# Reordering the split of weights in a hybrid decoder layer: low parts behind their sums, accumulating copies first, and three smaller moves

## The chip, the cores and the metric

The kernel runs on one core of a Trainium2 chip. The metric is the time of one execution on the device in microseconds; the time before is the median of three runs. The engines are named as in the profile: PE (TensorE, matrix products; its weight loads are PEld), DVE (VectorE), ACT (ScalarE), POOL (GpSimd) and SP (SyncE), which here only issues transfers.

## The reference

A decoder layer on 256 tokens of width 2048, all in float32. In short:

```python
h = layer_norm(ALPHA * x + 0.5 * swiglu(x, ffn1_w_in, ffn1_w_out))       # first feed-forward, width 5632
q, k, v, qi, ki, wi, rx, rg, gates = split_cols(h @ w_in)
y_attn = dsa_attention(rope(q), rope(k), v, rope(qi), rope(ki), wi)      # 64 keys of each query, by an indexer
y_rnn = rglru_branch(rx, rg, ...)                                        # short convolution, gates, linear recurrence
g_attn, g_rnn = split(sigmoid(gates))
merged = g_attn * (y_attn @ w_attn_branch) + g_rnn * (y_rnn @ w_rnn_branch)
h = layer_norm(ALPHA * h + merged @ w_out)
h = layer_norm(ALPHA * h + 0.5 * swiglu(h, ffn2_w_in, ffn2_w_out))       # second feed-forward
```

Here `swiglu(h, w_in, w_out)` is `(silu(a) * b) @ w_out`, with `a, b` the halves of `h @ w_in`.

## The kernel before

Every float32 product is made of three products of a rounded type (`F32R`): each operand is split into a high part, its rounded copy, and a low part, the rest; PE multiplies high by high, high by low and low by high. So each weight must be rounded by ACT (line 307) and subtracted by DVE (line 181) before PE can use it. The weights stream through in `pieces` of up to 1024 columns. `Weights.unit` hands PE the next piece and, at each new piece, loads pieces further ahead and splits pieces up to `AHEAD` = 4 ahead of the current one, into five buffers (`hl`).

Many blocks of 512 output columns use a scheme with seven instead of eight block products on quarters of an operand (a "chunk"). A chunk of weights (`rf`, 1024 KB) then gives four pieces, the forms of `FORMS`, and `operand` makes the sums that they need on DVE: `p1q3` a sum of 1024 columns into `ws` (line 262), `p2` one of 512 (266), `q5p7` one of 512 (269); `q4p6` needs none of its own, its operand being the results of 269 (first half) and 266 (second half). `p1q3` and `p2` round a part of the raw chunk, `q5p7` rounds `ws`.

A feed-forward has 22 blocks (`PLANS`). From block 6 on a block holds four pieces `o` of the product with `w_out`, for g tiles made earlier (`FILLS`), and 16 others: in three blocks out of four, four fast chunks; in the fourth, three chunks and two plain pieces `c`. At the end of a block `gate` adds its partial sums on DVE (lines 1209 to 1217, after ACT's copy in 1208), applies Silu on ACT, multiplies, and some pieces later transposes the result on PE and splits it into `g`. When four `o` pieces of an output block are done, `fill` copies two accumulators to `yd` on ACT (1250) and adds them to DRAM by a POOL transfer.

Some `o` pieces are `far`: they take no work of DVE. ACT writes a negated copy of the raw tile's half (207), a transfer on POOL's queue adds the weights to it from DRAM (208), which gives the low part, and ACT makes the rounded copy (212). A far piece has four such steps; `far_to` takes one step at each new piece, beginning 14 pieces ahead, and `far_steps` holds one generator for each piece, so that a piece is finished before the next begins.

PE, SP and POOL always run their instructions in the order of the program. DVE and ACT follow a planner's order, except in blocks 2 to 21 of each feed-forward (`WRITTEN`), where their order is the program's too. In these blocks `W.behind` is 1: the low part of a piece is put off until the next piece's sum and rounding have been issued (`lows`, `low_to`). Outside them `behind` is 0.

After the first feed-forward, `consts` computes in small steps the tables of the rotation and the constants of the recurrence (`hba`, `hbx`, `sp2`, `sp4`), while the last output product and the norm run. Later `merge` transposes each block of the merged branches and splits it (`split_two`) for the product with `w_out`; the last block (`nb` 3) is needed by the first block of that product.

Of the kernel before, what the change touches and what calls it, by code (L numbers as in the profile page):

```python
# [11 lines left out]
AF = mybir.ActivationFunctionType  # L12
# [130 lines left out]
class Weights:  # L143
# [8 lines left out]
    def __init__(self, nc, pool, pieces, on_piece):  # L152
        self.nc, self.pool, self.on_piece = nc, pool, on_piece
        self.fast_pool = self.third = None
        self.chunks = 0
        self.wide = None
        self.pieces = pieces
        self.raw = {}
        self.sums = {}
        self.hl = {}  # L160
        self.loaded = 0
        self.split = 0
        self.cur = -1
        self.limit = None
        self.cap = len(pieces)
        self.off = 0
        self.far = []
        self.soon = ()
        self.apart = ()
        self.far_raw = {}  # L170
        self.far_loaded = self.far_split = 0
        self.far_steps = deque()
        self.lows = deque()
        self.behind = 0

    def low_to(self, n):


        while len(self.lows) > n:
            lp, src, hp = self.lows.popleft()  # L180
            self.last = self.nc.vector.tensor_tensor(lp, src, hp, op=OP.subtract)  # L181

    def far_to(self, i):


        nc = self.nc
        while (self.far_loaded < len(self.far) and
               self.far[self.far_loaded] <= i + FAR_LOADS[self.far[self.far_loaded] in self.soon]):
            k = self.far[self.far_loaded]
            ap = self.pieces[k][0]  # L190
            t = self.far_raw[k] = self.pool.tile([P, PIECE], F32, name=f"raw{k}", tag="raw", bufs=RAW_BUFS)
            nc.sync.dma_start(t, ap)
            self.far_loaded += 1
        while self.far_split < len(self.far) and self.far[self.far_split] <= i:
            k = self.far[self.far_split]
            ap, t = self.pieces[k][0], self.far_raw.pop(k)
            self.far_split += 1
            self.far_steps.append((k, self.far_copies(k, ap, t)))
        if self.far_steps:
            self.far_step()  # L200

    def far_copies(self, k, ap, t):
        nc = self.nc
        h, l = [], []
        for c in range(2):
            l.append(self.wide())
            nc.scalar.activation(l[c], t[:, c * 512:(c + 1) * 512], AF.Copy, scale=-1.0)
            nc.gpsimd.dma_start(l[c], ap[:, c * 512:(c + 1) * 512], accum_op=OP.add)
            yield
        for c in range(2):  # L210
            h.append(self.wide())
            nc.scalar.activation(h[c], t[:, c * 512:(c + 1) * 512], AF.Copy)
            if c == 0:
                yield
        self.hl[k] = (h, l)

    def far_step(self):
        if next(self.far_steps[0][1], self) is self:
            self.far_steps.popleft()

    def key(self, i):
        ap, form = self.pieces[i]
# [55 lines left out]
    def split_to(self, i, step=PIECE):  # L278
        nc = self.nc
        while self.split <= min(i, len(self.pieces) - 1):  # L280
            form = self.pieces[self.split][1]
            if self.split in self.far:
                self.split += 1
                continue
            self.load_to(self.split)
            k = self.key(self.split)
            if self.split in self.apart:
                h, l = ([self.wide() for _ in range(2)] for _ in range(2))
                for c in range(2):
                    src = self.raw[k][:, c * 512:(c + 1) * 512]  # L290
                    nc.scalar.activation(h[c], src, AF.Copy)
                    nc.vector.tensor_tensor(l[c], src, h[c], op=OP.subtract)
                self.hl[self.split] = (h, l)
                del self.raw[k]
                self.split += 1
                continue
            hl = self.pool.tile([P, HL_PITCH], F32R, name=f"hl{self.split}", tag="hl", bufs=HL_BUFS)
            o = self.begin(self.split)
            h, l = hl[:, o:o + PIECE], hl[:, o + PIECE:o + 2 * PIECE]
            n = self.size(self.split)  # L300
            if form:
                parts = [(self.operand(k, form), *(x[:, :n].rearrange("p (f r c) -> p f r c", r=2, c=256)
                                                   for x in (h, l)))]
            else:
                parts = [tuple(x[:, q:min(n, q + step)] for x in (self.raw[k], h, l)) for q in range(0, n, step)]
            for src, hp, lp in parts:
                nc.scalar.activation(hp, src, AF.Copy)  # L307
                self.lows.append((lp, src, hp))
                self.low_to(self.behind)
            self.hl[self.split] = (h, l)  # L310
            if form in (None, FORMS[-1]):
                del self.raw[k]
            self.split += 1

    def unit(self, n):
        if self.cur < 0 or self.off == self.size(self.cur):
            self.hl.pop(self.cur, None)
            self.cur += 1
            self.off = 0
            self.far_to(self.cur + EARLY)  # L320
            while self.far_steps and self.far_steps[0][0] <= self.cur:
                self.far_step()
            self.load_to(self.cur + AHEAD + LOADS)
            self.split_to(self.limit or min(self.cur + AHEAD, self.cap))
            self.on_piece(self.size(self.cur) * (1 if self.pieces[self.cur][1] else 2))
        h, l = self.hl[self.cur]
        o = self.off
        self.off += n
        assert self.off <= self.size(self.cur)
        if self.cur in self.apart or self.cur in self.far:  # L330
            return h[o // 512], l[o // 512]
        return h[:, o:o + n], l[:, o:o + n]
# [80 lines left out]
def tile_layer(ctx, tc, x_fm, x_tm, pos, f1a, f1o, wA, wki, wB, wG, lru, wab, wrb, wo, f2a, f2o,  # L413
# [193 lines left out]
    def consts():  # L607
# [9 lines left out]
        for dst, turn, shift in ((sn, 0.0, 0.0), (cs, 0.25, 1.5707963267948966)):  # L617
            k = SM(32)
            r = SM(32)
            V.tensor_scalar(k, ang, 0.15915494309189535, turn, op0=OP.mult, op1=OP.add)  # L620
            V.tensor_scalar(k, k, 12582912.0, None, op0=OP.add)
            V.tensor_scalar(k, k, 12582912.0, None, op0=OP.subtract)
            V.scalar_tensor_tensor(r, k, -6.28125, ang, op0=OP.mult, op1=OP.add)
            V.scalar_tensor_tensor(r, k, -0.0019350051879882812, r, op0=OP.mult, op1=OP.add)
            yield
            V.scalar_tensor_tensor(r, k, -3.019916050195849e-07, r, op0=OP.mult, op1=OP.add)
            V.tensor_scalar(r, r, shift, None, op0=OP.add)
            V.tensor_scalar(r, r, 3.1415925, -3.1415925, op0=OP.min, op1=OP.max)
            angles.append((dst, r))
            yield  # L630
        o, w = COLS["ba"]
        V.tensor_scalar(hba, cols[:, o:o + w], 0.5, None, op0=OP.mult)
        o, w = COLS["bx"]
# [11 lines left out]
        V.tensor_scalar(n, ya, 1.4426950408889634, 12582912.0, op0=OP.mult, op1=OP.add)  # L645
        V.tensor_scalar(n, n, 12582912.0, None, op0=OP.subtract)
        yield
        with tc.issue_after(split.last.ins):
            for dst, r in angles:
                A.activation(dst.rearrange("p a b -> p (a b)"), r, AF.Sin)  # L650
        r = SM(NR)
        V.scalar_tensor_tensor(r, n, 0.693359375, ya, op0=OP.mult, op1=OP.subtract)
        V.scalar_tensor_tensor(r, n, -0.00021219444005469057, r, op0=OP.mult, op1=OP.add)
# [546 lines left out]
    def ffn(x, forms, ln):  # L1200
        def gate(c, e, g, i, lag, plain, steps):
# [4 lines left out]
            if e:  # L1206
                p1, p6, p7, q5 = e[0][:, :S], e[0][:, S:], e[1][:, :S], e[1][:, S:]
                A.activation(z4[:, 0], p1, AF.Copy)
                V.tensor_tensor(z4[:, 1], z4[:, 0], p6, op=OP.add)
                if lag != LAG_T[1]:  # L1210
                    W.low_to(0)
                V.tensor_tensor(z4[:, 2], z4[:, 1], p7, op=OP.add)
                V.tensor_tensor(b, q5[:, None, :].to_broadcast([P, 2, S]), z4[:, 1:3], op=OP.subtract)
                for t in range(2):
# [39 lines left out]
        for s, (b0, b1) in enumerate(SEGS):  # L1254
            for n in range(b0, b1):
                if n == WRITTEN[0]:
                    ordered.enter_context(tc.manual_schedule(
                        engines={mybir.EngineType.DVE, mybir.EngineType.Activation}))
                    W.behind = 1
                if n == NBK - 1:  # L1260
                    W.cap = W.cur + len(PLANS[n]) + 2
                c, e = blockF(x, forms, PLANS[n], fill)
# [3 lines left out]
                    next(task)  # L1266
                W.cap = len(pieces)
                bg.add("gate", task)
        W.behind = 0
        W.low_to(0)  # L1270
        ordered.close()

        def back():
# [311 lines left out]
        return r  # L1585

    bg.add("rope", indexer(1))
    for h in range(NH):
        bg.add("head", head(h), 4, PIECE)
    for b in range(6):  # L1590
# [106 lines left out]
    def merge(s, nb):  # L1697
# [3 lines left out]
        for c2 in range(2):  # L1701
            ps = BP()
            for c in range(2):
                for t in range(2):
                    T.transpose(ps[:, c * S + t * P:c * S + (t + 1) * P],
                                s[t][:, (2 * c2 + c) * P:(2 * c2 + c + 1) * P], ident)
            mg[4 * nb + 2 * c2], mg[4 * nb + 2 * c2 + 1] = split_two("mg", ps)

    for nb in range(4):
        if nb == 2:  # L1710
# [105 lines left out]
```

## Time and profile before

| | us |
|---|---|
| median of three runs (lowest to highest) | 2291.48 (2288.58 to 2291.97) |
| profiled execution: time | 2290.86 |
| profiled execution: span, first to last instruction | 2289.1 |
| PE busy | 2235.5 |
| DVE busy | 2146.3 |
| ACT busy | 1553.1 |
| POOL busy | 307.5 |

The granted PE clock is 0.998 of full speed. By time the first feed-forward's blocks run to about 650 us, its output product and norm to 705; the projections and attention to about 1160, the recurrence to about 1400, the branch products to 1500, the output product and the second norm to 1610, and the second feed-forward's blocks to about 2235. Matrix products are pipelined, so a row shows one of 256 columns as 0.28 us long, though one starts every 0.11 us; 512 columns show 0.38 and start every 0.22. On DVE and ACT successive instructions overlap in the same way by some 0.1 us. In a row of the timeline the bracket gives the engine's idle time before the instruction and what ended it; in a row of the waits stand the total, the number of times and the longest.

### The profile page before, as it was taken

How to read it: one execution, taken by the hardware profiler on the slowest of the kernel's cores; microseconds unless marked ns; L12 is line 12 of the kernel's file. 1: busy time of each engine (PE TensorE's matmuls, PEld its weight loads, DVE VectorE, ACT ScalarE, POOL GpSimd, SP SyncE). 2: the span in 40 equal slices, each digit the busy share in tenths (PEclk: the TensorE clock that was granted, in tenths of full speed). 3: DMA queues.
4: the chain of work that ended last, by engine and by line, in shares of the span. 5: the costliest groups of instructions: out<-in, count | busy, mean ns of one | idle time of the engine just before them, and what ended most of it. 6: DMA issues, size and time to landing. Idle time of an engine off the chain costs nothing.

```text
span 2289.1 us, 39930 instructions
## 1 busy us (share of the span) xinstructions
PE 2235.5 (98%) x15214; PEld 2071.1 (90%) x15214; DVE 2146.3 (94%) x3121; ACT 1553.1 (68%) x2270; POOL 307.5 (13%) x416
## 2 busy tenths in 40 slices
PE   9999999999999999999999999999999999999998
PEld 7999999999988999889999998888889899999997
DVE  8999999999989999979988889998999999999997
ACT  7666777777757656566557885546667677777773
POOL 1111222222210000000100002100111122222211
PEclk9999999999999999999999999999999999999999
DMA  9878999898966555664676668756787899999975
GB/s 364 260 223 233 293 270 294 249 295 256 300 223 220 197 175 204 217 203 147 248 250 205 208 193 306 256 186 212 265 272 216 247 265 279 272 270 294 268 236 205
DMA packets 150959, 559.52 MB, mean 244 GB/s; under 512 B 17616, under 2 KB 18384, under 8 KB 127856
## 3 DMA queue, kind: packets, MB, share of 16 engines
q1 hardware_dynamic: 102672, 455.00, 55.2%
q0 software_dynamic: 47952, 101.85, 21.9%
q8 instruction: 119, 1.95, 0.3%
q14 instruction: 72, 0.59, 0.1%
q10 hardware_dynamic: 144, 0.13, 0.0%
HBM read 519.69 MB, written 37.22 MB: 243 GB/s over the span
## 4 chain that ended last, share of the span: by engine, by line
PE 36%; DVE 24%; issue 6%; DMA 2%; ACT 1%; POOL 0%; DVEq 0%; ACTq 0%; POOLq 0%
PE mm L802 20%; DVE hl L181 12%; PE mm L1479 9%; PE bp L802 6%; DVE ws L262 3%; DMA wd<-f2o 1%; DVE rf L266 1%; DVE rf L269 1%; ACT hl L307 1%; PE bp L1479 1%; DVE z L1217 1%; DMA rf<-wrb 0%; DVE y L777 0%; DVE y L775 0%; DVE stg L1369 0%
## 5 line engine op out<-in xcount | busy, mean ns | idle before, releaser
L307 ACT ACTIVATE hl<-rf 128x1024 fp32r<-128x1024 f32 x537 | 484.4, 912 | 249.5 <-DVE rf L269 128.9
L181 DVE TENSOR_TENSOR hl<-rf,hl 128x1024 fp32r<-128x1024 f32 x537 | 557.8, 1040 | 2.4 <-ACT hl L307 1.9
L181 DVE TENSOR_TENSOR hl<-raw,hl 128x1024 fp32r<-128x1024 f32 (+2 forms) x403 | 475.0, 1190 | 52.7 <-ACT hl L307 50.9
L307 ACT ACTIVATE hl<-raw 128x1024 fp32r<-128x1024 f32 (+2 forms) x403 | 410.6, 1032 | 164.4 <-PE mm L802 113.9
L802 PE MATMUL mm<-hl,hs 128*128 128x512 f32 (+1 forms) x2532 | 498.5, 337 | 11.8 <-DVE hl L181 6.7
L802 PEld LDWEIGHTS mm<-hl,hs 128*128 128x128 f32 x2532 | 410.0, 190 | 56.4 <-DVE hl L181 9.1
L802 PE MATMUL bp<-hl,sh 128*128 128x256 f32 x2148 | 429.6, 276 | 0.4 <-DVE hl L181 0.4
L802 PEld LDWEIGHTS bp<-hl,sh 128*128 128x128 f32 x2148 | 354.6, 192 | 1.4 <-DVE hl L181 0.6
L802 PE MATMUL mm<-wd,g 128*128 128x512 f32 x1176 | 267.2, 379 | 6.6 <-DMA wd<-f2o 4.2
L802 PE MATMUL bp<-hl,sl 128*128 128x256 f32 x1074 | 258.4, 275 | 0.0
L802 PEld LDWEIGHTS mm<-wd,g 128*128 128x128 f32 x1176 | 218.1, 189 | 39.7 <-DMA wd<-f2o 6.5
L802 PE MATMUL mm<-hl,xs 128*128 128x256 f32 (+1 forms) x1272 | 231.6, 316 | 15.0 <-DVE hl L181 8.9
L262 DVE TENSOR_TENSOR ws<-rf 128x1024 f32<-128x1024 f32 x179 | 218.3, 1220 | 8.7 <-DMA rf<-wrb 3.7
L307 ACT ACTIVATE hl<-ws 128x1024 fp32r<-128x1024 f32 x179 | 188.7, 1054 | 52.5 <-DVE ws L262 16.6
L802 PEld LDWEIGHTS mm<-hl,xs 128*128 128x128 f32 x1272 | 193.3, 192 | 30.9 <-DVE hl L181 11.6
L1479 PE MATMUL mm<-hs,hl 128*128 128x256 f32 x1920 | 219.5, 275 | 0.0
L181 DVE TENSOR_TENSOR hl<-ws,hl 128x1024 fp32r<-128x1024 f32 x179 | 218.0, 1218 | 1.2 <-ACT hl L307 1.1
L802 PE MATMUL mm<-hl,g 128*128 128x512 f32 (+1 forms) x936 | 212.9, 381 | 4.8 <-DVE hl L181 4.3
L1479 PEld LDWEIGHTS mm<-hs,hl 128*128 128x128 f32 x1920 | 216.6, 192 | 0.3
L802 PEld LDWEIGHTS bp<-hl,sl 128*128 128x128 f32 x1074 | 206.1, 192 | 0.8
L802 PEld LDWEIGHTS mm<-hl,g 128*128 128x128 f32 x936 | 173.5, 191 | 29.3 <-DVE hl L181 5.5
L802 PE MATMUL mm<-hl,sh 128*128 128x256 f32 x716 | 158.4, 275 | 0.0
(278 smaller groups left out, 3060.2 us busy)
## 6 DMA issues: line engine op xcount, KB each, us to landing
rf<-f1a SPq DMA_DIRECT2D x70, 1024.0 KB, 8.0
rf<-f2a SPq DMA_DIRECT2D x70, 1024.0 KB, 8.1
raw<-f1o SPq DMA_DIRECT2D x88, 512.0 KB, 8.1
raw<-f2o SPq DMA_DIRECT2D x88, 512.0 KB, 7.9
raw<-wB SPq DMA_DIRECT2D x80, 512.0 KB, 4.9
raw<-wG SPq DMA_DIRECT2D x54, 512.0 KB, 4.6
wd<-f1o POOLq DMA_DIRECT2D x92, 256.0 KB, 9.0
wd<-f2o POOLq DMA_DIRECT2D x92, 256.0 KB, 8.9
```

The source lines that it names most:

```text
L181: self.last = self.nc.vector.tensor_tensor(lp, src, hp, op=OP.subtract)
L262: v.tensor_tensor(t, b[:, 0:4:3], b[:, 1:2].to_broadcast([P, 2, 2, 256]), op=OP.add)
L266: v.tensor_tensor(b[:, 1], t[:, 1], b[:, 0], op=OP.add)
L269: v.tensor_tensor(b[:, 0], b[:, 1], b[:, 2], op=OP.add)
L307: nc.scalar.activation(hp, src, AF.Copy)
L802: T.matmul(o, x, m, start=start, stop=stop)
L1217: V.tensor_tensor(zt, zt, c[t][:, :w], op=OP.add)
L1479: T.matmul(ps.rearrange("p (k e) -> p k e", e=2), w, x.rearrange("p (e k) -> p k e", e=2), start=start, stop=stop)
```

## The change

- `low_to`, `lows` and `behind` go: each low part is issued directly after its own sum and rounding, in the written blocks too, and `gate` no longer has one between its sums.
- The rounding of the form `q4p6` becomes two ACT instructions of half the size, the second half of the operand first.
- `far_steps` becomes two queues, one of negated copies with their accumulating transfers, one of rounded copies. Each step takes from the first as long as there is something in it. Still one step for each new piece, and all steps of a piece before it is current.
- `consts` ends after the rotation's tables. The rest is the generator `lru_consts`, begun with the attention heads, beside the gate products.
- The split of the last merged block is issued under `tc.high_priority()`.

```diff
@@ Weights
-        self.far_steps = deque()
-        self.lows = deque()
-        self.behind = 0
-    def low_to(self, n):
-        while len(self.lows) > n:
-            lp, src, hp = self.lows.popleft()
-            self.last = self.nc.vector.tensor_tensor(lp, src, hp, op=OP.subtract)
+        self.far_steps = deque(), deque()
@@ far_to, for each far piece that comes within reach
-            self.far_steps.append((k, self.far_copies(k, ap, t)))
+            h, l = self.hl[k] = [None] * 2, [None] * 2
+            for c in range(2):
+                part = slice(c * 512, (c + 1) * 512)
+                self.far_steps[0].append((k, self.far_low, (l, c, t[:, part], ap[:, part])))
+                self.far_steps[1].append((k, self.far_high, (h, c, t[:, part])))
+    def far_low(self, l, c, src, ap):
+        l[c] = self.wide()
+        self.nc.scalar.activation(l[c], src, AF.Copy, scale=-1.0)
+        self.nc.gpsimd.dma_start(l[c], ap, accum_op=OP.add)
+    def far_high(self, h, c, src):
+        h[c] = self.wide()
+        self.nc.scalar.activation(h[c], src, AF.Copy)
+    def far_step(self, until=None):
+        for steps in self.far_steps:
+            while steps and (until is None or steps[0][0] <= until):
+                _, step, args = steps.popleft()
+                step(*args)
+                if until is None:
+                    return
@@ split_to
-                nc.scalar.activation(hp, src, AF.Copy)
-                self.lows.append((lp, src, hp))
-                self.low_to(self.behind)
+                for r in (1, 0) if form == FORMS[-1] else (slice(None),):
+                    nc.scalar.activation(hp[:, r], src[:, r], AF.Copy)
+                self.last = nc.vector.tensor_tensor(lp, src, hp, op=OP.subtract)
@@ consts, and a new generator behind it
+    def lru_consts():
         o, w = COLS["ba"]
         V.tensor_scalar(hba, cols[:, o:o + w], 0.5, None, op0=OP.mult)
...
@@ gate
                 V.tensor_tensor(z4[:, 1], z4[:, 0], p6, op=OP.add)
-                if lag != LAG_T[1]:
-                    W.low_to(0)
                 V.tensor_tensor(z4[:, 2], z4[:, 1], p7, op=OP.add)
@@ ffn
-                    W.behind = 1
...
-        W.behind = 0
-        W.low_to(0)
@@ attention
     bg.add("rope", indexer(1))
+    bg.add("main", lru_consts())
@@ merge
-            mg[4 * nb + 2 * c2], mg[4 * nb + 2 * c2 + 1] = split_two("mg", ps)
+            with tc.high_priority() if nb == 3 else nullcontext():
+                mg[4 * nb + 2 * c2], mg[4 * nb + 2 * c2 + 1] = split_two("mg", ps)
```

More of the change, by code (lines that the diff above doesn't have):

```diff
@@ L197, in far_to @@
             self.far_split += 1
-            self.far_steps.append((k, self.far_copies(k, ap, t)))
[L199 to L219, printed above, removed]
+            h, l = self.hl[k] = [None] * 2, [None] * 2
[3 more added lines that the diff above has]
+                self.far_steps[1].append((k, self.far_high, (h, c, t[:, part])))
+        self.far_step()
+    def far_low(self, l, c, src, ap):
[12 more added lines that the diff above has]
+                    return
     def key(self, i):
@@ L320, in unit @@
             self.far_to(self.cur + EARLY)
-            while self.far_steps and self.far_steps[0][0] <= self.cur:
-                self.far_step()
+            self.far_step(self.cur)
             self.load_to(self.cur + AHEAD + LOADS)
@@ L630, in consts @@
             yield
+        with tc.issue_after(split.last.ins):
+            for dst, r in angles:
+                A.activation(dst.rearrange("p a b -> p (a b)"), r, AF.Sin)
+    def lru_consts():
         o, w = COLS["ba"]
@@ L647, in consts @@
         yield
-        with tc.issue_after(split.last.ins):
-            for dst, r in angles:
-                A.activation(dst.rearrange("p a b -> p (a b)"), r, AF.Sin)
         r = SM(NR)
```

## The prediction

> **What bounds the kernel now.** I read the windows of the two long feed-forward stretches first, then the waits of PE and of DVE inside them, then the timeline rows in which PE or DVE sat idle.
>
> ```profile
> core 0: us, PE busy (x) PEld busy (x) DVE busy (x) ACT busy (x) POOL busy (x), PEclk, DMA share, GB/s
> 60.00:650.00 590.00, 577.87 (x4084) 541.84 (x4082) 571.94 (x668) 432.43 (x605) 120.89 (x140) 1.00 0.90 262
> 1640.00:2215.00 575.00, 561.36 (x3961) 525.22 (x3959) 562.21 (x658) 422.26 (x593) 116.98 (x134) 1.00 0.91 268
> PE mm L802 <- DVE hl L181: 11.1, 15, 2.2
> PE mm L802 <- DMA wd<-f1o: 1.3, 2, 1.0
> PE mm L802 <- DVE hl L181: 6.7, 12, 1.3
> PE mm L802 <- DMA wd<-f2o: 4.2, 4, 1.5
> DVE hl L181 <- ACT hl L307: 5.3, 5, 1.6
> DVE z L1209 <- ACT z L1208: 8.5, 8, 2.0
> ```
>
> Half of the run lies in these two stretches, and there PE (98%) and DVE (97%) are both nearly full, ACT (73%) is not. PE lacks 12.1 us in the first and 13.6 in the second, DVE 18.1 and 12.8. So no gain here can pass 25.7 us, and it comes only if the idle time of the two engines is made to coincide less. The wait rows (two of PE in the first stretch, two of PE in the second, two of DVE in the first; the first stretch is taken to 655 there) say what PE lacks: mostly the low part (L181), then the accumulated copies (wd). The timeline shows where:
>
> ```profile
> 170.98 0.49 PE L802 MATMUL mm<-hl,xs 128*128 128x256 f32 x2 [1.32 <-DVE hl L181]
> 202.97 0.49 PE L802 MATMUL mm<-hl,xs 128*128 128x256 f32 x2 [1.32 <-DVE hl L181]
> 326.18 0.49 PE L802 MATMUL mm<-hl,xs 128*128 128x256 f32 x2 [0.85 <-DVE hl L181]
> 357.02 0.49 PE L802 MATMUL mm<-hl,xs 128*128 128x256 f32 x2 [0.84 <-DVE hl L181]
> 418.19 0.49 PE L802 MATMUL mm<-hl,xs 128*128 128x256 f32 x2 [0.35 <-DVE hl L181]
> 652.10 8.90 PE L802 MATMUL mm<-hl,g 128*128 128x512 f32 x40 [2.17 <-DVE hl L181]
> 401.15 0.42 DVE L1209 TENSOR_TENSOR z<-z,bp 128x256 f32<-128x256 f32 x1 [2.03 <-ACT z L1208]
> 401.49 1.22 DVE L181 TENSOR_TENSOR hl<-rf,hl 128x1024 fp32r<-128x1024 f32 x1
> 402.63 0.41 DVE L1212 TENSOR_TENSOR z<-z,bp 128x256 f32<-128x256 f32 x1
> 415.79 1.22 DVE L262 TENSOR_TENSOR ws<-rf 128x1024 f32<-128x1024 f32 x1
> 416.92 1.22 DVE L181 TENSOR_TENSOR hl<-rf,hl 128x1024 fp32r<-128x1024 f32 x1
> ```
>
> The gaps repeat once a block, at one place: the last two products of a q4p6 form, which need its low part. In the DVE rows that low part (416.92) stands behind the next chunk's first sum (415.79); the two starts lie 1.13 us apart, and PE's gap of 0.35 ends at 418.19, as the low part does. The other loss is at a block's end: DVE waits 2.03 us for the first gate sum (401.15) while a low part that is already rounded stands behind it (401.49).
>
> **The change part by part.** The sum is made against the profiled execution, 2290.86 us (span 2289.1), 0.6 below the median shown, 2291.48.
>
> *1. Low parts directly behind their sums.* In blocks 2 to 21 of both feed-forwards the same DVE instructions run in another order. At the gap the low part comes one sum (1.13) earlier. At a block's end where DVE is idle, a second low part (1.13) moves into the idle time ahead of the gate sum. Together 2.27 us of lead over the walk from one place to the other. From the second I take off 0.4, because that low part will itself wait for its rounding, so 1.9. Is the lead used up? A cycle is four blocks, three with four fast chunks and one with three. Gap to gap a block takes 357.02-326.18 = 30.84, of which PE idles 0.85: DVE loses about 0.85 on PE with each fast block, 2.5 over three, and the fourth gives it back. A lead of 1.9 therefore covers all but some 0.3 to 0.8 of a cycle's gaps; take 0.5 left. In the first cycle (170.98, 202.97) a block takes 31.99 and PE idles 1.49 of it (1.32 and one smaller gap), 4.5 in three blocks; there the lead saves 1.9 and the rest stays, since DVE has no idle time to give. The two stretches have 8.9 (11.1 less the 2.17 at 652.10) and 6.7 us of such gaps: 4.5 each are the first cycle's, 6.6 the six later cycles'. Gain: 2 x 1.9, and 6.6 - 6 x 0.25 (half of what is left was DMA's, below) = 5.1. Together 8.9; bounds 0 (DVE's work per block is unchanged, so where it has no idle time nothing need come) and 15.6 (all).
>
> The price is a wait that was hidden: a low part that follows its own sum waits for ACT where ACT is late. The place is the block's fill end:
>
> ```profile
> 395.83 1.09 ACT L1250 ACTIVATE yd<-mm 128x512 f32<-128x512 f32 x2 [1.64 <-PE mm L802]
> 397.90 1.23 DVE L181 TENSOR_TENSOR hl<-raw,hl 128x1024 fp32r<-128x1024 f32 x1 [0.87 <-ACT hl L307]
> ACT hl L307 <- DVE rf L269: 128.9, 110, 3.7
> L307 ACT ACTIVATE hl<-rf 128x1024 fp32r<-128x1024 f32 x358 | 375.2, 1056 | 206.4 <-DVE rf L269 128.9 <-PE mm L802 52.7 <-PE bp L802 13.9
> L307 ACT ACTIVATE hl<-rf 128x512 fp32r<-128x512 f32 x179 | 111.9, 625 | 43.0 <-PE mm L802 40.4 <-PE mm L785 1.7 <-PE bp L802 0.5
> ```
>
> ACT's copies to yd wait for PE, and the next rounding stands behind them. Now DVE has a sum to do meanwhile; afterwards it waits up to one sum (1.13) more. There are 40 pairs of such copies. Mostly PE is then the late one and the lead of 1.9 bears it, so I take a net 3 us of loss, between 0 and 40 x 1.13 = 45.
>
> *2. The last form rounded in halves.* The rounding of q4p6 waits for the sum at L269 (128.9 us, 110 times). Half of its operand is ready a sum earlier, so only the second half (625 ns) is left behind that sum, and it ends within the low part of the form before (1.22): without halves, 1056 ns would barely fit. That removes a new wait of part 1 more than one of today. Cost: 179 x (2 x 625 - 1056) = 35 us of ACT work at most, in an engine that idles 27%. Zero, 0 to 2.
>
> *3. Negated copies ahead of rounded ones.* Two far pieces lie side by side; the second one's negated copies now come before the first one's rounded copies, two steps earlier.
>
> ```profile
> 1915.04 0.62 ACT L207 ACTIVATE wd<-raw 128x512 fp32r<-128x512 f32 x1
> 1918.14 0.63 ACT L207 ACTIVATE wd<-raw 128x512 fp32r<-128x512 f32 x1
> 1919.15 1.59 POOL L208 DMA_DIRECT2D wd<-f2o x1
> 1935.11 0.70 PE L802 MATMUL mm<-wd,g 128*128 128x512 f32 x2 [1.22 <-DMA wd<-f2o]
> DMA to landing us min/median/max: 4.0/9.0/16.2
> SPq L248 <- ACT wd L212: 15.4, 5, 6.2
> SPq L248 <- DVE hl L181: 484.5, 74, 14.9
> ```
>
> PE's gap at 1935.11 is at the last two products of the second far piece, whose second negated copy ran at 1918.14; its accumulating DMA is POOL's row at 1919.15, issued behind two yd stores, and lands 16 us later. The copy would take the place of a rounded one some 4 us earlier, and POOL would issue it ahead of the yd stores. The longest such wait is 1.5, so these gaps (1.3 + 4.2) should go: 5.5. I count 5.0 (0 to 6). The same number of copies runs on ACT, and POOL issues as many DMAs. The rounded copies come later, but still several pieces ahead of PE. The raw tile of the first piece is freed two steps later, so SP's queue, where a load waits for it five times (15.4), waits some 3 us more at each; that is covered, as SP waits 484.5 us for DVE anyway. If that cover goes, a load of rf is late next and DVE's first sum waits for it.
>
> The Trainium skill, DMA: Bandwidth & Descriptors, section on the anatomy of one DMA issued from GpSimd, fits a single transfer as a fixed 2 us plus its bytes over 436 GB/s; for 256 KB that is an estimate of 2.6 us. By it the copy of 1918.14 would have landed near 1923, no order of copies would matter, and this term would be 0. The landing row above, median 9.0, disagrees, and the measurement decides.
>
> *4. The last merged tile split with priority.*
>
> ```profile
> 1507.42 1.04 PE L1705 MATMUL bp<-ident,gf 128*128 128x128 f32 x8
> 1514.35 0.63 ACT L707 ACTIVATE sh<-sf 128x512 fp32r<-128x512 f32 x1 [3.23 <-DVE sf L705]
> 1515.83 1.07 ACT L956 ACTIVATE mg<-bp 128x512 fp32r<-128x512 f32 x2
> 1516.46 0.48 PE L802 MATMUL mm<-hl,mg 128*128 128x512 f32 x1 [2.82 <-ACT mg L956]
> 1517.83 9.51 PE L802 MATMUL mm<-hl,mg 128*128 128x512 f32 x35 [0.89 <-DVE mg L957]
> ```
>
> The transposes end at 1508.5, but ACT copies them only at 1515.83, after it sat 3.23 us behind a subtraction of another task. Put first, the copies end near 1509.6 and DVE's halves near 1511, ahead of PE's need at 1513.6: 3.7 goes. ACT's roundings move back by 1.07 and DVE's low parts by 1.3, which five buffers ahead cover. Gain 3.3 (0 to 3.7). Late next is the low part of a weight piece.
>
> *5. The recurrence constants beside the gates.*
>
> ```profile
> 685.75 0.18 DVE L675 TENSOR_TENSOR s<-s,s 128x20 f32<-128x20 f32 x1
> 689.53 1.12 PE L1007 MATMUL bp<-ident,y 128*128 128x128 f32 x8 [0.81 <-DVE y L1027]
> ```
>
> By the code 49 tiny DVE instructions leave the end of the first feed-forward; each 0.18, so up to 9 us of DVE. A few stand within the norm's chain ahead of the gap of 0.81. Gain 0.5 (0 to 1.5). They land in the gate products, where heads and low parts leave DVE idle in the trace; 0 (a loss of up to 1).
>
> *6. Ends of the feed-forwards.* At 652.10 PE waits 2.17 for a low part behind the gate sums, which stand behind another low part. That one now runs earlier; DVE's sums end about 0.7 sooner. Twice: 1.4 (0 to 2.2).
>
> Sum: 8.9 - 3 + 0 + 5.0 + 3.3 + 0.5 + 1.4 = 16.1 of gain. 2290.86 - 16.1 = 2274.8; on the scale of the median 2275.4. I predict 2275.
>
> **Rivals.**
> *A, slower.* The hidden wait of part 1 is paid in full: at each block's fill DVE stands a whole sum behind ACT. For it: 0.87 at 397.90, already exposed with a sum in front. Against it: only 5.3 us of such waits in the first stretch. Price 45 us, less the 19.1 of gains: 2291.5 + 26 = 2317. It decides from 19.1/40 = 0.48 us a pair; at 0.6 the time is 2296.
> *B, half of it.* The new order only swaps the gate wait for a rounding wait, and DVE's work per block, 30.84 where PE needs 30.0, keeps setting the blocks' pace. Then part 1 nets 2 and the DMA gaps, in which DVE now catches up, turn into low part gaps (2 instead of 5): 9 us of gain, 2282.5.
> *C, no change.* The stretches stay DVE's altogether and part 1's price eats part 3; parts 4 to 6 alone, less a loss from another order of ACT and DVE outside the written blocks: 2288 or so.
>
> **How the numbers follow.** 0.2% is 4.6 us, about what a measurement of this kernel can tell from no change: faster is below 2286.9, slower above 2296.1. Forecast 0.56 (its own range 2268 to 2280), B 0.22, C 0.13, A 0.09. Faster is the forecast, B and a little of C: 0.80; same most of C and the mild end of A: 0.13; slower 0.07. The range runs from 2265, near where all gaps named (15.6 + 6 + 3.7 + 1.5 + 2.2 = 29) less a price of 3 would go, to 2288, which leaves out A and half of C.
>
> **What would show it.** Right: the low part starts directly behind its own sum; the gaps of 0.85 at q4p6 are gone and the 1.32 ones smaller; no PE gap on wd; mg copied right behind the transposes; the wait of L1209 for ACT smaller. Wrong: DVE's waits for ACT's rounding in the two stretches grow past 20 us, PE's gaps at low parts stay near 15, or DVE's first sums begin to wait for rf loads.

## The result and the profile after

The changed kernel takes 2271.26 us (2269.62 to 2280.3), the kernel before 2290.69 (2288.58 to 2291.97) beside it: a ratio of 0.9925, 95% interval 0.991 to 0.9939. Forecast were 2275 and a gain of 16; it is 19.4. The profiled execution has a span of 2268.8 us, 20.3 less than before.

The page of the changed kernel, busy times (before: PE 2235.5, DVE 2146.3, ACT 1553.1 us with 2270 instructions):

```profile
PE 2230.7 (98%) x15214; PEld 2070.9 (91%) x15214; DVE 2134.7 (94%) x3121; ACT 1580.2 (70%) x2449; POOL 306.2 (13%) x416
```

ACT has 179 instructions more, the second halves, and 27 us more work. The same windows of the two feed-forwards as in the prediction, and the waits of DVE and PE in the first (60 to 655, the first four lines) and the second (the last two); a wait row is: engine, tile, line <- what ended it: us in all, times, the longest.

```profile
60.00:650.00 590.00, 585.99 (x4135) 550.85 (x4134) 575.97 (x696) 448.61 (x680) 120.30 (x140) 1.00 0.91 269
1640.00:2215.00 575.00, 567.75 (x4033) 533.50 (x4032) 563.10 (x665) 439.21 (x670) 120.32 (x141) 1.00 0.91 266
DVE hl L302 <- ACT hl L301: 11.9, 16, 1.5
PE bp L796 <- DVE hl L302: 2.9, 9, 0.4
PE mm L796 <- DVE z L1209: 0.3, 1, 0.3
DVE z L1203 <- ACT z L1202: 0.3, 1, 0.3
DVE hl L302 <- ACT hl L301: 8.9, 13, 1.2
PE bp L796 <- DVE hl L302: 3.2, 10, 0.4
```

PE now lacks 4.0 and 7.3 us (12.1 and 13.6 before). Its waits for low parts fell from 11.1 to 2.9 and from 6.7 to 3.2; those for wd are gone (its largest wait left in the second is 2.2 for g, 0.5 before); DVE's gate wait fell from 8.5 to 0.3; DVE's wait for roundings rose from 5.3 to 11.9. Where the time came from is read from PE's transposes, which both kernels issue in one order. Before, then after: ends of two blocks four blocks apart, the last gate transposes of the first feed-forward, the first norm (its row of before, 689.53, stands in the prediction), the start of the second feed-forward's norm output, and the last gate transposes of the second.

```profile
288.80 0.60 PE L1233 MATMUL bp<-ident,z 128*128 128x128 f32 x4
411.66 0.60 PE L1233 MATMUL bp<-ident,z 128*128 128x128 f32 x4
660.84 0.60 PE L1233 MATMUL bp<-ident,z 128*128 128x128 f32 x4
1600.63 1.04 PE L1041 MATMUL bp<-ident,y 128*128 128x128 f32 x8
2248.75 0.60 PE L1233 MATMUL bp<-ident,z 128*128 128x128 f32 x4
```

```profile
287.44 0.60 PE L1225 MATMUL bp<-ident,z 128*128 128x128 f32 x4
407.11 0.60 PE L1225 MATMUL bp<-ident,z 128*128 128x128 f32 x4
648.31 0.60 PE L1225 MATMUL bp<-ident,z 128*128 128x128 f32 x4
676.20 1.04 PE L1001 MATMUL bp<-ident,y 128*128 128x128 f32 x8
1590.81 1.04 PE L1035 MATMUL bp<-ident,y 128*128 128x128 f32 x8
2226.80 0.60 PE L1225 MATMUL bp<-ident,z 128*128 128x128 f32 x4
```

The first feed-forward gains 12.5 us, the second 12.1 (the lead grows from 9.8 to 21.95), the first norm 0.8; the stretch from there to the second feed-forward loses 3.5 (13.3 to 9.8), and the tail 1.65 (the spans differ by 20.3). Between the first and the last gate transposes of each feed-forward PE's idle time falls from 14.2 to 4.0 and from 15.8 to 7.3, 18.8 of these 24.6 us. The granted clock enters two of the figures: the run of 2280.3 us had 0.987 where the other three had 0.997 to 0.998, and in the profile of before it was 0.50 for 3.4 us from 2239 on, in a last block that took 34.75 us where the same block of the first feed-forward took 33.06, so that 1.7 of the second one's 12.1 is the clock's.

The gain is not the same in each cycle of four blocks. The cycle shown (blocks 10 to 13) takes 119.67 us instead of 122.86, 3.2 less. A block is taken here from the transposes behind the block before to its own, and blocks are counted from 0. By such rows the first cycle (6 to 9) gains 1.3 in each feed-forward, the next two 3.2 each in the first and 2.6 and 2.4 in the second, and the last four blocks 4.8 and, without the clock's 1.7, 4.9.

### The profile page after: what moved, and what is told of

It is laid out like the page before. It is cut to its first block, busy times and chain, and to the rows that moved or that the text cites. A ratio compares the mean times of both kernels' runs of the same rounds, so it can differ in the third digit from the quotient of the medians.

```text
span 2268.8 us, 40241 instructions
## 1 busy us (share of the span) xinstructions
PE 2230.7 (98%) x15214; PEld 2070.9 (91%) x15214; DVE 2134.7 (94%) x3121; ACT 1580.2 (70%) x2449; POOL 306.2 (13%) x416
## 4 chain that ended last, share of the span: by engine, by line
PE 40%; DVE 20%; issue 5%; ACT 2%; DMA 1%; POOL 0%; DVEq 0%; ACTq 0%; POOLq 0%
PE mm L796 24%; DVE hl L302 10%; PE mm L1468 7%; PE bp L796 7%; DVE ws L255 2%; DVE rf L262 1%; ACT hl L301 1%; DVE rf L259 1%; DMA raw<-f2o 1%; PE bp L1468 1%; DMA ya<-yd 0%; DVE stg L1358 0%; DVE sl L702 0%; ACT f L1024 0%; PE bp L1225 0%
## 5 line engine op out<-in xcount | busy, mean ns | idle before, releaser
L301 ACT ACTIVATE hl<-rf 128x1024 fp32r<-128x1024 f32 x716 | 516.8, 734 | 185.0 <-PE mm L796 71.3
L301 ACT ACTIVATE hl<-ws 128x1024 fp32r<-128x1024 f32 x179 | 188.9, 1056 | 76.0 <-DVE ws L255 46.7
```

The lines of the kernel that those rows point to most:

```text
L301: nc.scalar.activation(hp[:, r], src[:, r], AF.Copy)
```

## The experiments

**One part alone.** The kernel before with the low parts directly behind their sums, q4p6 rounded whole:

```
-                    W.behind = 1        # stays 0: nothing lags
```

> The kernel before with one edit: each low part directly behind its own sum in the written blocks (q4p6 still rounded whole, copies in the old order, constants and merge as before). Theory L (the order of DVE carries the gain of the feed-forwards): PE's gaps at low parts fall from 8.9 and 6.7 us to under 4 each, the gaps on wd stay, the two feed-forwards together get some 13 us shorter, so about 2278. Theory C (the earlier accumulating copies carry it): under 4 us of gain, above 2286. Theory P (the hidden wait for the rounding is a real price, which only the halves take away): DVE's waits for ACT's rounding in the two stretches rise above 20 us and the time is 2285 or more.

2291.35 us, ratio 0.9999 (0.9989 to 1.0009): nothing. The halves alone, low parts left one behind:

```
-                nc.scalar.activation(hp, src, AF.Copy)
+                for r in (1, 0) if form == FORMS[-1] else (slice(None),):
+                    nc.scalar.activation(hp[:, r], src[:, r], AF.Copy)
```

> The kernel before with one edit: q4p6 rounded in halves, low parts still one sum behind. Theory J (halves and direct low parts work only together: the lag already hides the rounding): within 2 us of the kernel before. Rival (ACT's late rounding costs by itself and the halves carry the gain): 8 us or more faster, 2283 or less.

2290.48 us, ratio 0.9993 (0.9983 to 1.0002): nothing either. Both edits together:

> The run above plus the rounding of q4p6 in halves. Theory L as forecast: the halves cost and gain nearly nothing, within 3 us of the run above. Theory P: at least 6 us faster than the run above, with DVE's waits for ACT's rounding that much smaller.

2271.57 us, ratio 0.9907 (0.9892 to 0.9922): about 20 us, the whole gain of the change. Two parts that are worth nothing apart are worth 20 together. The reason stands in DVE's timeline, and not in the list of waits. A chunk before, then the same in the changed kernel with the rounding on ACT (start, duration):

```profile
418.06 0.68 DVE L266 TENSOR_TENSOR rf<-ws,rf 128x512 f32<-128x512 f32 x1
418.66 1.22 DVE L181 TENSOR_TENSOR hl<-rf,hl 128x1024 fp32r<-128x1024 f32 x1
419.91 0.69 DVE L269 TENSOR_TENSOR rf<-rf 128x512 f32<-128x512 f32 x1
```

```profile
412.60 1.22 DVE L302 TENSOR_TENSOR hl<-rf,hl 128x1024 fp32r<-128x1024 f32 x1
413.74 0.68 DVE L259 TENSOR_TENSOR rf<-ws,rf 128x512 f32<-128x512 f32 x1
414.34 0.69 DVE L302 TENSOR_TENSOR hl<-rf,hl 128x512 fp32r<-128x512 f32 x1
414.94 0.68 DVE L262 TENSOR_TENSOR rf<-rf 128x512 f32<-128x512 f32 x1
415.54 1.22 DVE L302 TENSOR_TENSOR hl<-ws,hl 128x1024 fp32r<-128x1024 f32 x1
415.66 0.63 ACT L301 ACTIVATE hl<-rf 128x512 fp32r<-128x512 f32 x1 [0.29 <-DVE rf L262]
416.68 1.22 DVE L302 TENSOR_TENSOR hl<-rf,hl 128x1024 fp32r<-128x1024 f32 x1
```

A row of 1.22 is normally followed after 1.13 to 1.14 (412.60 to 413.74): neighbours overlap by 0.09. Before, the sum at L269 overwrites, in rf, what the low part right ahead of it reads; it starts only when that has ended, 1.25 behind it (418.66 to 419.91). Neither row shows a wait, and both count as busy throughout. In the changed order two 512-column instructions lie between (413.74 and 414.34). The Trainium skill, Perfetto Trace Analysis, section on the per-instruction lifecycle of a DVE or Act instruction, says that the next instruction may begin its prefetch once the one before has finished executing, while a semaphore is signalled only when the writes are acknowledged, where the profiler ends the row; the 1.13 and 1.25 agree. Another page of the Trainium skill, VectorE: DVE Perf Modes, section on the DRAIN you can't avoid, measured that a semaphore behind each of eight copies costs nothing extra; it doesn't say that one copy needed another's data, and here a neighbour that needs to wait for the one ahead costs 0.12 us.

And the first part alone, in the same place:

```profile
413.57 0.69 DVE L269 TENSOR_TENSOR rf<-rf 128x512 f32<-128x512 f32 x1
414.18 1.22 DVE L181 TENSOR_TENSOR hl<-ws,hl 128x1024 fp32r<-128x1024 f32 x1
414.38 1.06 ACT L307 ACTIVATE hl<-rf 128x1024 fp32r<-128x1024 f32 x1 [1.80 <-DVE rf L269]
415.47 1.23 DVE L181 TENSOR_TENSOR hl<-rf,hl 128x1024 fp32r<-128x1024 f32 x1
```

The whole rounding starts 0.12 behind the sum's end and ends at 415.44; the low part starts at 415.47, 1.29 behind its neighbour. So 0.155 is lost here in place of the 0.12 there, and by the account below some 0.16 at 119 such places, 19 us. Again no row shows a wait, as the low part ahead ended only 0.07 before.

To count this, I took for each two neighbouring DVE rows of the two stretches (60 to 640, 1640 to 2200; rows that the listing joins left out) the distance of their starts, less the usual distance behind a row of that form (the lowest tenth in the changed kernel), and added up what is over 0.04 us, by cause:

| us of DVE lost | behind a neighbour's read or write | gate sums | roundings | other | all | time |
|---|---|---|---|---|---|---|
| before | 19.6 | 17.8 | 4.6 | 1.2 | 43.2 | 2290.7 |
| low parts direct | 0 | 1.0 | 39.7 | 0.7 | 41.4 | 2291.4 |
| halves alone | 18.9 | 17.6 | 4.9 | 0 | 41.4 | 2290.5 |
| both | 0 | 1.0 | 24.5 | 0.5 | 26.0 | 2271.6 |
| changed | 0 | 1.0 | 21.5 | 0.6 | 23.1 | 2271.3 |

The figures are good to about 1.5 us, by which they move when the usual distance is taken a little differently. The column "all" and the time move together: 17.2 and 20 us from before to both, 20.1 and 19.4 to the changed kernel, and nearly nothing for either part alone. In part this is arithmetic. In each of the cycles of blocks 10 to 17 DVE runs the same instructions, 117.0 to 117.8 us of them in all these kernels, and the cycle lasts for these plus what DVE loses, whichever engine makes it wait. So the account says where the time went, and it doesn't prove which loss set the pace. In the changed kernel PE idles only 0.4 of the 119.7 us of such a cycle: there PE sets the pace, and the 2.3 us that DVE still loses cost next to nothing.

**Does the neighbour's overlap carry time by itself?** The changed kernel with p2's low part moved behind the next sum, so that two sums of which the second reads what the first wrote stand side by side:

```
+                self.lows.append((lp, src, hp))
+                while self.lows and form != "p2":
+                    lp, src, hp = self.lows.popleft()
                     self.last = nc.vector.tensor_tensor(lp, src, hp, op=OP.subtract)
```

> The changed kernel, with the low part of p2 moved behind the sum of q5p7, so that two sums of which the second reads what the first wrote stand next to each other on DVE in each chunk; the low part of p2 runs one 512-column instruction (0.60 us) later, all else as in the changed kernel. Theory K, overlap: the second sum starts only after the first has ended, 0.72 us behind its start instead of 0.60, in some 128 chunks of the two stretches: 15 us of DVE time, in stretches where DVE is 98% full: 2283 (2278 to 2288). Theory S (only the place of the low parts counts): a low part that comes 0.6 us later, several pieces ahead of its use, costs nothing: 2271 (2269 to 2273).

2280.80 us, ratio 0.9956 (0.9939 to 0.9973): 9.5 slower than the changed kernel's 2271.26. Its timeline:

```profile
332.03 0.69 DVE L260 TENSOR_TENSOR rf<-ws,rf 128x512 f32<-128x512 f32 x1
332.75 0.69 DVE L263 TENSOR_TENSOR rf<-rf 128x512 f32<-128x512 f32 x1
333.36 0.69 DVE L306 TENSOR_TENSOR hl<-rf,hl 128x512 fp32r<-128x512 f32 x1
334.10 0.49 PE L800 MATMUL mm<-hl,xs 128*128 128x256 f32 x2 [0.77 <-DVE hl L306]
```

0.72 between the sums, 0.61 between the unrelated neighbours. By the account, 119 such pairs lose 14.3 us, the roundings 5 less than in the changed kernel, all 33.6: 10.5 more than there, for 9.5 us of time. Theory K's number came out, but the run doesn't isolate its cause. The edit also puts the low part of p2 later, by 0.72 (a sum of 0.60 and the 0.12), and that is where PE now waits: the low part of 333.36 ends at 334.05, and PE's gap of 0.77 ends at 334.10. 25 of PE's gaps in the two stretches, 16.5 us of some 21, end so, 18 of them with 0.77; in the changed kernel no gap of PE ends with p2's low part. So theory S's "several pieces ahead of its use" was wrong, and the delay has a price of its own.

Blocks 6 and 7 show the pairs alone: there DVE loses 0.48 us a block, all of it to four pairs, and a block takes 31.93 us, where the changed kernel loses 0.31 to roundings and takes 31.75. Where DVE waits for nothing else, the time of a pair is time of the kernel. How the 9.5 us divide between pairs and delay stays open.

**The opposite test missed.** The kernel before with only q4p6's low part one behind, which parts the pair at L269 without the halves:

```
-                self.low_to(self.behind)
+                self.low_to(self.behind if form in (None, FORMS[-1]) else 0)
```

> The kernel before, in which only the last form's low part (q4p6) still goes one step behind, past the next chunk's first sum; the low parts of p1q3, p2 and q5p7 stand directly behind their own sums. q4p6 is rounded whole. Theory K, overlap: in the trace of before the sum at L269 overwrites what the low part directly ahead of it reads, and the two starts lie 1.252 us apart, 90 times in the two stretches, where the same low part ahead of an unrelated instruction (L266) takes 1.135: 0.117 lost each time, shown as no wait. Here no such pair is left at L269, and no new wait for a rounding comes, since q4p6's rounding still has a whole sum to hide behind. DVE loses 10.5 us less in the two stretches, and the time falls by 8 to 13: 2281 (2278 to 2284). Theory S, the prediction's reading (PE's gaps come because q4p6's low part stands behind the next chunk's first sum): that low part stays exactly there, so the gaps stay: 2291 (2289 to 2293).

2298.77 us, ratio 1.0031 (1.002 to 1.0041): slower, against both theories. The pairs at L269 are gone (3.9 us of neighbours' loss is left, at ws), but DVE meets another wait. DVE and ACT at the block's feed of g, and PE's wait for low parts in 60 to 640:

```profile
322.57 1.23 DVE L181 TENSOR_TENSOR hl<-ws,hl 128x1024 fp32r<-128x1024 f32 x1
322.77 1.06 ACT L307 ACTIVATE hl<-rf 128x1024 fp32r<-128x1024 f32 x1 [2.26 <-DVE rf L269]
323.74 0.58 ACT L956 ACTIVATE g<-bp 128x512 fp32r<-128x512 f32 x1
324.35 0.69 DVE L957 TENSOR_TENSOR g<-bp,g 128x512 fp32r<-128x512 f32 x1 [0.56 <-ACT g L956]
PE mm L802 <- DVE hl L181: 11.3, 10, 1.9
```

DVE's subtraction for g waits for ACT's copy of g, and this stands behind q4p6's rounding. 24 times 0.65 us are 15.6 us; roundings take 16.7, and all of DVE's loss is 44.5, 1.3 over before. That says why nothing was gained. PE's waits for low parts, nearly all for q4p6's, grew besides, from 8.9 to 11.3 in this window and from 6.7 to 10.3 in the second stretch: theory S named the place rightly, and was too low. In the profiled executions, which lie 4.8 us apart (2295.65 and 2290.86), the two feed-forwards are 1.8 and 2.2 us longer from the first to the last gate transposes, and PE idles 1.7 and 3.2 more in them. Why the medians differ by 7 stays open.

**The order of the copies.** The kernel before with part 3 alone (negated copies of all far pieces in one queue ahead of the rounded ones, as in the change's diff):

> The kernel before with one edit: negated copies with their accumulating transfers ahead of the rounded copies. Theory L: PE's gaps on wd (1.3 and 4.2 us) vanish, but in them DVE caught up, so part of them comes back as gaps at low parts: 2 to 4 us faster, about 2288. Theory C: 10 us or more faster, 2281 or less.

2291.33 us, ratio 0.9996 (0.9986 to 1.0005). Its waits of PE in 60 to 640, and that of "both", where the copies are still in the old order:

```profile
PE mm L803 <- DVE hl L181: 10.6, 15, 1.3
```

```profile
PE mm L803 <- DMA wd<-f1o: 3.0, 3, 2.5
```

The waits for wd are gone, 1.3 us, and the waits for low parts went from 8.9 in this window to 10.6: refilled, as DVE is late. In its trace the two feed-forwards are 1.7 and 0.3 us shorter than before and the stretch between them is longer, so a gain too small for the interval (3 us) is not excluded. In "both" PE waits for wd 2.5 us at one place; the changed kernel has no such wait. The changed kernel's last gate transposes of the first feed-forward lie 2.4 earlier (648.31, 650.74 in "both", which had begun 0.3 ahead), and its second feed-forward is 0.4 shorter. So part 3 is worth some 3 us once DVE is no longer late, and nothing that the times show before. The changed kernel without part 5, below, takes 2267.47, 4.1 less than "both", for parts 3 and 4 together.

**The constants.** The changed kernel without part 5:

```
-    bg.add("main", lru_consts())         # its body back at the end of consts()
```

> The changed kernel with the recurrence constants computed where they were, behind the rotation tables at the end of the first feed-forward. Theory H (the planner hoists the 47 small instructions into the projections, where DVE is full, and they cost PE time there): the projections get some 4.8 us shorter, the first norm some 0.9 longer, about 2267. Rival (the loss in the projections is another order of the planner's and not the constants): within 1.5 us of the changed kernel, 2271.

2267.47 us, ratio 0.9891 (0.9876 to 0.9906): part 5 costs 3.8. One window of the projections, before, then changed, then the latter's two largest gaps of PE, and one of the moved instructions:

```profile
760.00:930.00 170.00, 168.09 (x1341) 161.54 (x1340) 168.28 (x303) 103.19 (x138) 3.30 (x6) 1.00 0.60 211
```

```profile
760.00:930.00 170.00, 164.16 (x1297) 156.45 (x1296) 169.14 (x331) 101.64 (x145) 2.71 (x5) 1.00 0.56 196
804.40 2.40 PE L796 MATMUL mm<-hl,hs 128*128 128x512 f32 x10 [1.49 <-DVE bias L1418]
837.00 2.40 PE L796 MATMUL mm<-hl,hs 128*128 128x512 f32 x10 [1.90 <-DVE stg L1358]
L673 DVE TENSOR_SCALAR sp<-s x1: 169/169/169, 862.7 to 862.7; 128x20 f32<-128x20 f32 x1
```

The planner ran 47 of the 49 small instructions between 793.4 and 862.8, in the projections, where DVE is busy 99% of the time, and not beside the gate products for which the program names them. PE lost 3.9 us of busy time there, as theory H held. Held back until the feed-forward's last split instruction:

```
+    bg.add("main", later(lru_consts(), W.last.ins))
```

> The changed kernel with the recurrence constants held back: none of their instructions may be issued before the low part that was last when the gate products begin. Theory H (the planner's early place costs the projections, the place itself is free): the projections regain some 4.8 us and the first norm keeps its 0.9, so 2266, a little under the run with the constants put back (2267.5). Rival (the gate products have no room for them either): 2269 or more.

2268.04 us, ratio 0.9897 (0.9882 to 0.9912): the same as with the constants in their old place. The projections are free again and the gates pay some 2.

**The last merged tile.** In addition a pause of two steps of the background task that splits mg's sums, so that in the program its rounding stands behind mg's copies:

```
+            for _ in range(pause if k == 0 else 0):   # pause=2 for mg
+                yield
```

> As the run above, and the left operands of the merged tiles, whose rounding holds ACT up, wait two steps more after the first pair, so that ACT's copies of the last merged block stand ahead of them in the program. Theory M (priority did nothing because the copies stood behind instructions issued earlier in the program; the stall is ACT's order): PE's gaps of 2.8 and 0.6 to 0.9 at the last merged block fall below 1 together, 2.5 to 3.5 us faster than the run above. Rival (the next wait takes their place, at the low parts or at the delayed left operands): within 1 us of it.

2265.52 us, ratio 0.9885 (0.9871 to 0.99). In the changed kernel, PE and ACT at that place:

```profile
1503.62 0.63 ACT L701 ACTIVATE sh<-sf 128x512 fp32r<-128x512 f32 x1 [3.23 <-DVE sf L699]
1505.10 1.07 ACT L950 ACTIVATE mg<-bp 128x512 fp32r<-128x512 f32 x2
1505.73 0.79 PE L796 MATMUL mm<-hl,mg 128*128 128x512 f32 x1 [2.82 <-ACT mg L950]
```

The same 3.23 and 2.82 us as before the change: the priority moved nothing. ACT's instruction that waits 3.23 for DVE still stands ahead of the copies. With the pause the gap is gone, and 2.5 us with it.

**One more far piece.** The changed kernel with a third piece of each group's fills made "far" from the second group on (its low part then comes from ACT and an accumulating DMA and not from DVE):

```
-                if k in (2, 6) and (g or nb >= 2) or k == 4 and g >= 2:
+                if k in (2, 6) and (g or nb >= 2) or k == 4 and g >= 1:
```

> The changed kernel with one more far piece in each of blocks 6 to 9 of both feed-forwards (the third piece of an output block), so that DVE has one low part of 1.13 us less in each. Theory D (there DVE's work still sets the pace, 31.7 us a block where a later fast block takes some 29.7): PE's gaps at low parts in these blocks vanish, a block takes under 30.7, 3 to 4 us in each feed-forward, about 2264. Rival (another wait takes over: the two more tiles that the piece holds, or its transfers): within 2 us of the changed kernel or slower.

2263.32 us, ratio 0.9875 (0.9858 to 0.9891): 7.9 below the changed kernel. Where they come from is read in the trace of the next run. The two best sets, constants in their old place and constants late, each with the pause and this edit:

> The changed kernel with three edits together: constants back at the end of the first feed-forward, the last merged block's copies ahead of the later left operands, a third far piece in blocks 6 to 9. If the three gains stand beside one another (3.8, 2.0 and 8 us by the runs so far), 2258. By theory D a block among 6 to 9 takes under 30.7 us in the profile, and PE's gaps at low parts there are gone. Rival (the third piece's gain of 8 us is not in these blocks): the blocks keep their 31.7.

> The same with the constants held back to the gate products instead. If their place matters little once they are out of the projections, within 2 us of the run above; if the gate products pay for them as the profile of the earlier run suggests (some 2 us), and the first norm gains 0.9, some 1 us slower than it.

2257.99 us, ratio 0.9858 (0.9842 to 0.9874), and 2257.31, ratio 0.9853 (0.9838 to 0.9867). Both beat both kernels, by 33 and 13 us; between the two there is nothing. 8 low parts fewer run on DVE (3113 of its instructions, from 3121). The transposes behind blocks 5 and 9 in the set with the constants in their old place, and that behind block 5 in the changed kernel, whose 287.44 above is the one behind block 9:

```profile
164.19 0.60 PE L1225 MATMUL bp<-ident,z 128*128 128x128 f32 x4
284.90 0.60 PE L1225 MATMUL bp<-ident,z 128*128 128x128 f32 x4
```

```profile
162.48 0.63 PE L1225 MATMUL bp<-ident,z 128*128 128x128 f32 x4
```

Blocks 6 to 9 take 120.71 instead of 124.96 us, 4.25 less, and as much less in the second feed-forward: this is the whole gain. Blocks 6 and 7 take 30.08 and 30.29 where the changed kernel took 31.75. So theory D was right about the place, with a little more in each feed-forward than the 3 to 4 forecast, and its rival was wrong; PE's gaps at low parts in these blocks fell from 1.8 to 1.0 and did not vanish.

## Why the prediction was right in its total and wrong in its terms

The sum of 16.1 stood near the 19.4 measured because its errors cancel: parts 1, 2 and 6 were put 13 too low, parts 3, 4 and 5 together 10 too high. That the total came out is luck.

*Parts 1, 2 and 6: 8.9 - 3 + 0 + 1.4 = 7.3 forecast, about 20 measured.* Three steps failed. First, "DVE's work per block is unchanged": I read it from row durations, which don't show that a neighbour can start early or not; 19.6 us lay there. Second, term 2 was put at zero because "without halves 1056 ns would barely fit". It doesn't fit, by 0.155 us a chunk, some 19 us, and the price of part 1 alone was 35 us (39.7 against 4.6), near rival A's 45, and as large as the gain. Third, the price: with halves the roundings still cost 17 us more (21.5 against 4.6), not 3; it is borne since overlap (19.6) and gates (16.8) gave 36.4. In this account the gates' gain and the roundings' price cancel, which is the swap that rival B named; what is left is the overlap, which neither the sum nor a rival named. It is what the account says, and no run takes the overlap away by itself.

Of the marks of being right the one on mg's copies failed, and one mark of being wrong came: DVE's waits for rounding passed 20 us (11.9 and 8.9 in the changed kernel), and the time was won all the same. It was no good test the other way either: in the list the first part alone shows 10.1 and 7.5, far less than what it lost.

The mechanism named for the gain, the lead of 1.9 us against a gap of 0.85 that comes once a block, was too small a story: the first cycles gave 1.3 each where it had 1.9, and the later ones 2.4 to 3.2 where it had some 0.85. The last block of each feed-forward (part 6) gave 2.4 where it had 0.7. The gaps were what was left visible of DVE's slower pace.

*Part 3: 5.0 forecast, about 3 measured,* and 0 alone. Rival B named why: with DVE late, DMA gaps become low part gaps. As to the single transfer's 2.6 us cited there, the waits for wd that the order alone removed confirm that the landing row, and not that figure, had to be taken.

*Part 4: 3.3 forecast, 0 measured.* The failed step is "put first": the priority didn't lift the copies past the rounding that stands ahead of them on ACT and waits for DVE. The place was right and the size near, as the pause gained 2.5.

*Part 5: +0.5 forecast, -3.8 measured.* "They land in the gate products" was taken from the program's order. The norm did gain its 0.8; the projections lost more.

## What to carry to other kernels

Where an engine reads 97% busy, measure from start to start: a neighbour that overwrites or reads what was just used, and a wait shorter than the usual overlap, cost a tenth of a microsecond each time here and stand in no list of waits. Where two in-order engines feed each other, try a reorder together with the split that makes its latency fit, since each by itself may read as nothing. After moving work "beside" something, look where it ran.

## What the runs showed of the hardware

Neighbouring DVE instructions of 1024 fp32 columns start 1.135 us apart, and 1.252 when the second overwrites what the first reads; behind 512 columns, 0.60 and 0.72. Both differences are 0.12 us. The Trainium skill, Vector Engine (DVE) Microarchitecture Reference, section on measured stream behaviour on trn2, gives 1.0417 ns a column and about 75 ns after overlap, an estimate of 1.14 and 0.61; the independent neighbours agree, the dependent ones don't reach it. From the end of a DVE sum to the start of the rounding on ACT that needs it passed 0.12 us in the first part alone (414.26 to 414.38; median 0.115 of 128), but 0.04 in the changed kernel (415.62 to 415.66; median 0.035 of 140); why they differ is open. From the rounding's end to the low part on DVE that waited for it passed 0.03 in both.
